# A decoder trunk on one Trainium2 core: norm weights loaded first, decay steps later, the residual's second half summed and turned by VectorE

## The chip, the cores and the metric

The kernel runs on one core of one Trainium2 chip. A core has TensorE (PE in the profile; its weight loads are listed apart as PEld), VectorE (DVE), ScalarE (ACT), GpSimd (POOL) and SyncE (SP), and 16 DMA engines, to which SP, ACT and POOL issue transfers. SBUF is the on-chip memory of 128 partitions, PSUM the memory that TensorE writes to. The metric is the device time of one execution in microseconds, as the median of several runs.

## The reference: what is computed

One layer of a decoder trunk on 1024 positions of width 1024, all in float32. Its core:

```python
h = rms_norm(x, g_mix[l])
z = jnp.einsum("bsd,de->bse", h, w_in[l]) + b_in[l]
va, ga, xb, gb, sa, sb = jnp.split(z, cuts, axis=-1)
u = va * jax.nn.sigmoid(ga)
u = causal_depthwise_conv(u, conv_a_w[l], conv_a_b[l])          # width 31
u = jax.nn.silu(layer_norm(u, ln_g[l], ln_b[l]))
y_a = jnp.einsum("bsc,cd->bsd", u, w_a_out[l])
v = causal_depthwise_conv(xb, conv_b_w[l], conv_b_b[l])         # width 4
v = rg_lru(v, w_rg_a[l], b_rg_a[l], w_rg_x[l], b_rg_x[l], lam[l])
y_b = jnp.einsum("bsc,cd->bsd", v * jax.nn.gelu(gb), w_b_out[l])
m = jax.nn.sigmoid(sa) * y_a + jax.nn.sigmoid(sb) * y_b
x = x + jnp.einsum("bsd,de->bse", m, w_o[l])

h = rms_norm(x, g_mlp[l])
f = jnp.square(jax.nn.relu(jnp.einsum("bsd,df->bsf", h, w_1[l])))
x = x + jnp.einsum("bsf,fd->bsd", f, w_2[l])
return rms_norm(x, g_final)
```

`rms_norm` divides each position by the root of its mean square (plus 1e-6) and multiplies by channel weights. The decay of the recurrence `rg_lru` needs `softplus(-lam)` for 1536 channels, which depends on the weights alone.

## The kernel before

**Layout and precision.** Activations lie with channels on the partitions and positions along the free dimension, in tiles of 128 x 1024 (two blocks of 512). Each float32 operand of a product is split into a high and a low part (`split`, `split_dma`, `low`), and a product is three matmuls: high times high, high times low, low times high. `split_dma` lets POOL form the low part by an accumulating DMA; the other two use VectorE. The larger products work in blocks of two by two with seven partial products, so that sums of blocks are formed on VectorE in between.

**Order of the work.** Nearly all of it is written out by hand: inside `tc.manual_schedule` the named engines run their instructions in the program's order. In most parts these are all five engines; in the first part (the start) and in the two parts of the MLP they are ScalarE, VectorE and TensorE only, and the order of SP and POOL is left to a scheduler. `later` puts VectorE work aside with a due time from a hand-kept clock (`clk`, advanced by `at`), and `vector_work` issues what was put aside. An engine runs its own instructions in order and waits where an input isn't there yet.

**The start (lines 107 to 422).** `vecs` is one array of 448 channel vectors of 128; its first eight are the norm weights `g_mix`. They are loaded alone into `gmix` by ACT's queue (L169), and the whole of it into `vec` by POOL (L130), behind the making of `ident` and the constants `onesm` and `ones`. `idle_mm` runs ten matmuls of `ones` on TensorE. `x_plain` (L236) multiplies a transposed x part by its norm weight and rounds it to the high part `xh`, `x_plain_low` (L240) makes the low part `xl`, and `first_z` (L274) issues the first products from them. The first half of the positions goes through TensorE without its root; for the second half `x_square` (L202 on VectorE for tile 6, L204 on ScalarE) sums the squares of rows, `x_root` (L211 and on) takes the root and forms diagonal tiles `rd`, and `x_spread` (L226) spreads them over all partitions with matmuls into `rb`. Between them `decay_on(n)` issues the next `n` of the 51 small VectorE operations of `decay` (128 x 12 elements each): 6, 14 and 5 at the start, the rest in step 5 of the first loop over output chunks (its index is `s`; each step is one output chunk of 128 channels).

**The residual and its norm (lines 1400 to 1660, steps `GX`).** The products named `a`, `o` and `u` are the convolution branch's output product, the output projection `w_o`, and the beginning of the MLP's first product. Each runs in seven groups, in the order `GORD`, of four matmul sets of twelve; `o0` is the first step of `o` and `u0 = 2 * o0` the first of `u`. The dictionary `GX` says what is issued behind the matmuls of a step. `x1[k, o, c2]` is the residual; `o` is 0 for even and 1 for odd positions, called the first and the second half here. `x1_second` makes the pieces of the second half: of group 5 (steps `o0 + 20` to `23`) and of group 3 (steps `o0 + 24` to `27`), each with one VectorE addition at the beginning of the next step.

For the first half the sums of squares go this way: `x1_sq` squares a piece on ScalarE (L1545), `x1_add` adds it up on VectorE, `x1_cols` (L1574) sums over partitions by four matmuls with a column of ones, `x1_root` and `x1_diag` take the root and make diagonal tiles, `x1_spread` (L1637) spreads them, `x1_normed` multiplies the residual by them and by the norm weights, in place. The residual is also needed as rows at the end: `x1_turn` turns it by VectorE in blocks of 32 x 32, and `x1_rows_out` writes it to `x1d` in DRAM, four DMAs a call with pieces of 512 bytes.

For the second half `x1_rows` does both: 32 transposes on TensorE (L1587) into PSUM, squares from there with the sums along the row on ScalarE (L1592), eight copies out of PSUM on VectorE (L1596), four DMAs of whole rows (L1600).

**The MLP's first product (steps `useq`, extra work in `UX`).** The block `i` of w_1 is loaded by `up_load` (L1679), its sums and splits are made by `up_lhs`, and `up_step` runs the matmuls and empties PSUM. Loads, operands, the residual and its norm all take their tiles from one pool `T` of 37 tiles of 128 x 1024.

Of the kernel before, what the change touches and what calls it, by code (L numbers as in the profile page):

```python
# [9 lines left out]
F32 = mybir.dt.float32  # L10
# [3 lines left out]
ALU = mybir.AluOpType  # L14
# [16 lines left out]
def trunk_kernel(ctx: ExitStack, tc: tile.TileContext, x, xt_in, xt_eo, vecs, w_in, w_a_out, w_b_pl, w_b_sq,  # L31
# [74 lines left out]

    ident = cp.tile([P, P], F32, name="ident")
# [4 lines left out]
    ones = cp.tile([P, P], F32, name="ones")  # L112
    nc.gpsimd.memset(ones, 1.0)
# [14 lines left out]

    gmix = cp.tile([P, 16], F32, name="gmix")
    nc.gpsimd.dma_start(vec, vecs)  # L130
# [38 lines left out]
    nc.scalar.dma_start(gmix[:, 0:8], vecs[:, 0:8])  # L169
# [8 lines left out]
    for t in range(4, 8):  # L178
        load_x(t)
    for c2 in range(4):  # L180
        load_xc(1, c2)
# [169 lines left out]
    with tc.manual_schedule(engines={mybir.EngineType.Activation, mybir.EngineType.DVE,  # L351
# [30 lines left out]
        decay_on(6)  # L382
# [4 lines left out]
        decay_on(14)  # L387
# [34 lines left out]
        nc.vector.tensor_tensor(csum, pairs[:, :, 0, :], pairs[:, :, 1, :], ALU.add)  # L422

# [405 lines left out]
    with tc.manual_schedule(engines=ENGINES):  # L829
        for s in range(3, NC1):  # L830
# [48 lines left out]
            if s == 5:  # L879
                decay_on()  # L880
# [662 lines left out]
    def x1_sq(i, m_):  # L1543
        s = EV(f"sq{i}{m_}")
        nc.scalar.activation(s, x1[i // 2, 0, i % 2][:, HALVES[m_]], AF.Square)  # L1545
        sqs.append((at("A", 0.62, clk["V"]), s))
# [6 lines left out]
    def x1_turn(kk):  # L1553
        for th in range(2):
            r = T(f"x1r{kk}{th}")
            for c2 in range(2):
                src = x1[kk, 0, c2].rearrange("p (m h b j) -> p h m b j", m=2, h=2, j=32)[:, th]
                dst = r.rearrange("p (b m j) -> p m b j", m=4, j=32)[:, 2 * c2:2 * c2 + 2]
                dve(0.65, 0, nc.vector.transpose, dst, src)
            turned.append((kk, th, r))  # L1560

    turned = []
# [15 lines left out]
    def x1_rows(*ts):  # L1578
        for t in ts:
            o, n = divmod(t, 4)  # L1580
            if n == 0:
                rst[o] = cp.tile([P, 6, 4], F32, tag="st6", name=f"stm{o}", bufs=2)
            rows = T(f"x1r{t}")
            for kk in range(2):
                ps = bank(f"tr{t}{kk}")
                for c in range(4):
                    nc.tensor.transpose(ps[:, c * P:(c + 1) * P],  # L1587
                                        x1[kk, o, c // 2][:, c % 2 * HS + n * P:c % 2 * HS + (n + 1) * P],
                                        ident)
                at("P", 0.45)  # L1590
                a = T(f"sq{t}{kk}")[:, 0:HS]
                nc.scalar.activation(a, ps, AF.Square, accum_out=rst[o][:, kk, n:n + 1])  # L1592
                at("A", 0.63, clk["P"])

                def copy(rows, kk, ps, t):
                    nc.vector.tensor_copy(  # L1596
                        rows[:, HALVES[kk]].rearrange("p (g c j) -> p c g j", g=4, c=4),
                        ps.rearrange("p (c g j) -> p c g j", g=4, c=4))
                    if kk:
                        nc.sync.dma_start(x1d[t], rows)  # L1600

                later(clk["P"], 0.63, copy, rows, kk, ps, t)
            if t == 7:
                x1_root(1)
            if o:
                vector_work(clk["V"])

    def x1_root(o):

        if o == 0:  # L1610
            rst[o] = cp.tile([P, 6, 4], F32, tag="st6", name=f"stm{o}", bufs=2)
        a, b, v, s = (rst[o][:, i, :] for i in range(4))
        if o:
            tt(v, a, b, ALU.add)
        nc.vector.tensor_scalar(v, v if o else sqs[1][:, 0:4], 1.0 / D, EPS, ALU.mult, ALU.add)
        nc.scalar.activation(s, v, AF.Sqrt)
        at("A", 1.5)
# [679 lines left out]
```

## Time and profile before

| | |
|---|---|
| Median of 3 runs | 1528.98 us (1528.98 to 1529.56) |
| The profiled execution's own time | 1529.02 us |
| Its span, first to last instruction | 1527.2 us |
| Mean granted clock of TensorE | 0.998 |
| TensorE busy | 1517.7 us |

A page of the profile lists busy times by engine, the share of 40 slices, the DMA queues, the chain of work that ended last, and the costliest groups of instructions. A row of the timeline reads: start, length, engine, line of the kernel, operation, output and inputs by tile names, shape, count, and in brackets how long the engine stood idle before it and what ended that. A tile name stands for all tiles whose name begins that way (`x1r` for `x1r00` and so on; `x` also for the tiles `x100` and the like of the residual). Helpers that record all operations have one line: L482 is `dve`, which issues most of VectorE's work in the later parts, L1236 is `low`, and L65 to L67 are `split_dma`. `SPq` and `ACTq` are DMA issues by these engines' sequencers. "us to landing" is from the issue until the last byte is in place.

### The profile page before, as it was taken

To read this page: it belongs to the slowest core of one execution; us is meant where nothing else is said; L and a number is where in the kernel's file an instruction comes from. 1 tells how busy PE (TensorE), PEld (TensorE's weight loads), DVE (VectorE), ACT (ScalarE), POOL (GpSimd) and SP (SyncE) were. 2 spreads that over 40 slices of the span, in tenths; PEclk is the share of its full clock that TensorE was granted. 3 is DMA by queue.
4 is the path that set the end of the run, shared out by engine and by line. 5 is a ranking of instruction groups with operands and counts; after the bars stand their busy time and mean duration, and the time that the engine had idled before them with its cause. 6 is when DMAs were issued, how large, how long until landed. Compare 5 with 4: busy or idle time off the path is not lost.

```text
span 1527.2 us, 18954 instructions
## 1 busy us (share of the span) xinstructions
PE 1517.7 (99%) x6712; PEld 1249.8 (82%) x6712; DVE 1200.8 (79%) x1640; ACT 927.0 (61%) x1299; POOL 192.3 (13%) x228
## 2 busy tenths in 40 slices
PE   9999999999999999999999999999999999999998
PEld 7878887888888888888888888888888888888886
DVE  7899996999999997788869879755555387777777
ACT  6749688586566657645575777554444455545475
POOL 0111011022222222000022322000000000101010
PEclk9999999999999999999999999999999999999999
DMA  9756778698997789863779897333333974776465
GB/s 352 187 145 159 176 177 191 193 260 213 266 260 173 186 207 273 292 231 121 263 205 302 186 200 189 124 126 111 111 111 111 307 261 129 187 201 167 110 123 153
DMA packets 130943, 295.48 MB, mean 193 GB/s; under 512 B 12912, under 2 KB 34928, under 8 KB 130848
## 3 DMA queue, kind: packets, MB, share of 16 engines
q1 hardware_dynamic: 98816, 214.60, 41.1%
q0 software_dynamic: 31600, 79.15, 28.2%
q8 instruction: 52, 0.85, 0.2%
q10 hardware_dynamic: 432, 0.53, 0.1%
q14 instruction: 43, 0.35, 0.1%
HBM read 148.74 MB, written 60.82 MB: 137 GB/s over the span
## 4 chain that ended last, share of the span: by engine, by line
PE 98%; DMA 1%; DVE 0%; issue 0%; SPq 0%; ACT 0%; DVEq 0%
PE z L745 16%; PE d1b L2017 2%; PE d2b L2017 2%; PE d0b L2017 2%; PE d3b L2017 2%; PE d0e L2017 1%; PE d0a L2017 1%; PE d3e L2017 1%; PE d3a L2017 1%; PE d1e L2017 1%; PE d1a L2017 1%; PE d2e L2017 1%; PE d2a L2017 1%; PE z L274 1%; PE rg L552 1%; PE rg L554 1%
## 5 line engine op out<-in xcount | busy, mean ns | idle before, releaser
L745 PE MATMUL z<-xh,win_h 128*128 128x512 f32 x368 | 115.5, 391 | 0.0
L745 PE MATMUL z<-xl,win_h 128*128 128x512 f32 x368 | 115.0, 390 | 0.0
L657 DVE SCALAR_TENSOR_TENSOR y<-u,vec,y 128x511 f32<-128x511 f32 (+14 forms) x120 | 88.2, 735 | 0.0
L745 PE MATMUL z<-xh,win_l 128*128 128x512 f32 x368 | 87.5, 390 | 0.0
L657 DVE SCALAR_TENSOR_TENSOR yt<-u,vec,yt 128x511 f32<-128x511 f32 (+6 forms) x112 | 82.4, 736 | 0.0
L657 DVE SCALAR_TENSOR_TENSOR y<-yt,csum,y 128x511 f32<-128x511 f32 (+6 forms) x112 | 82.4, 736 | 0.0
L745 PEld LDWEIGHTS z<-xh,win_h 128*128 128x128 f32 x368 | 69.1, 188 | 15.9 <-ACT win_h L67 0.5
L745 PEld LDWEIGHTS z<-xl,win_h 128*128 128x128 f32 x368 | 69.1, 188 | 14.9
L745 PEld LDWEIGHTS z<-xh,win_l 128*128 128x128 f32 x368 | 69.1, 188 | 14.6
L562 ACT ACTIVATE g<-rg,vec 96x1024 f32<-96x1024 f32 x32 | 35.5, 1110 | 72.9 <-PE rg L554 72.9
L1712 ACT ACTIVATE o<-s 128x512 fp32r<-128x512 f32 x56 | 33.7, 623 | 45.2 <-DVE s L1696 26.4
L66 POOL DMA_DIRECT2D zo<-zw x45 | 39.2, 871 | 134.7 <-ACT zo L65 116.8
L503 DVE SCALAR_TENSOR_TENSOR v<-xb,vec,v 128x1023 f32<-128x1023 f32 (+2 forms) x36 | 46.2, 1282 | 5.8 <-ACT v L494 4.9
L66 POOL DMA_DIRECT2D db_10l<-br x4 | 3.5, 876 | 338.3 <-DMA br<-in_w_dram 253.0
L66 POOL DMA_DIRECT2D win_l<-win_raw x23 | 20.0, 868 | 194.2 <-ACT win_l L65 159.4
L65 ACT ACTIVATE zo<-zw 128x512 fp32r<-128x512 f32 x45 | 28.2, 626 | 24.2 <-PE z2f L946 2.1
L1236 DVE TENSOR_TENSOR o<-s,o 128x512 fp32r<-128x512 f32 x56 | 37.3, 683 | 1.5 <-ACT o L1712 1.5
L66 POOL DMA_DIRECT2D zo<-zs x30 | 26.4, 879 | 74.9 <-ACT zo L65 62.8
L67 ACT ACTIVATE zo<-zw 128x512 fp32r<-128x512 f32 x45 | 27.9, 621 | 0.0
L598 DVE TENSOR_TENSOR_SCAN g<-a,g 128x1024 f32<-128x1024 f32 x12 | 27.5, 2291 | 0.4
L66 POOL DMA_DIRECT2D ga<-gsa x8 | 7.0, 874 | 161.0 <-DMA m<-mbd 150.8
L1236 DVE TENSOR_TENSOR o<-w_raw,o 128x512 fp32r<-128x512 f32 x38 | 25.9, 683 | 0.0
(3178 smaller groups left out, 4910.1 us busy)
## 6 DMA issues: line engine op xcount, KB each, us to landing
w_raw<-in_w_dram SPq DMA_DIRECT2D x32, 512.0 KB, 5.1
br<-in_w_dram SPq DMA_DIRECT2D x32, 512.0 KB, 5.8
ar<-fd SPq DMA_DIRECT2D x32, 512.0 KB, 6.6
zw<-in_w_in_dram SPq DMA_DIRECT2D x28, 512.0 KB, 6.9
win_raw<-in_w_in_dram SPq DMA_DIRECT2D x23, 512.0 KB, 4.6
win_l<-win_raw POOLq DMA_DIRECT2D x23, 512.0 KB, 4.8
zo<-zw POOLq DMA_DIRECT2D x45, 256.0 KB, 5.8
gates<-zg SPq DMA_DIRECT2D x32, 256.0 KB, 4.4
```

Of the source, the lines that this page charges most:

```text
L65: nc.scalar.activation(l, src, AF.Copy, scale=-1.0)
L66: nc.gpsimd.dma_start(l, src, accum_op=ALU.add)
L67: nc.scalar.activation(h, src, AF.Copy)
L274: nc.tensor.matmul(z0[i][:, HALVES[hf]], w0[i][w][:, k, :], xpart(a, hf, k), start=k == 0 and which == "hh", stop=k == 7 and which == ("hl ...
L503: nc.vector.scalar_tensor_tensor(v[:, d:S], a[:, 0:S - d], cbw_c[:, w * 12 + t:w * 12 + t + 1], v[:, d:S], ALU.mult, ALU.add)
L562: nc.scalar.activation(a, gps.pop((n, gi))[:HD, :], AF.Sigmoid, bias=(ba_c, bx_c)[gi][:, n:n + 1])
L598: nc.vector.tensor_tensor_scan(i, a, i, 0.0, ALU.mult, ALU.add)
L657: nc.vector.scalar_tensor_tensor(o[:, k:], a[:, 0:HS - k], c, o[:, k:], ALU.mult, add)
L745: nc.tensor.matmul(zps[s][:, HALVES[hf]], w[:, k, :], xw[k][part][hf], start=n == 0, stop=n == 23)
L1236: tt(l, src, h.bitcast(F32), ALU.subtract)
L1712: nc.scalar.activation(o[:, 0], src, AF.Copy)
L2017: nc.tensor.matmul(o, a, b, start=start and n == 0, stop=stop and n == len(todo) - 1, skip_group_check=not start or not stop)
```

## The change

1. `ones` is made first on POOL, and POOL then loads the norm weights into `gmix`; `ident` and `onesm` follow. ACT no longer loads them.
2. The whole of `vecs` is loaded by SP, behind x tiles 4 to 7 and ahead of the transposed x of the second part of positions.
3. The decay steps: none ahead of the first root; 5 at the end of the start, 27 in step 5, the others in step 6.
4. For the second half of the residual `x1_rows` is gone. Its squares and sums now go as those of the first half (`x1_sq`, `x1_add`, `x1_cols`), its rows by `x1_turn` in steps 12, 14, 16 and 18 of the first product, with `x1_rows_out` in steps 14 to 20.
5. The first half's rows are written right behind their turning (steps `o0 + 20` and `21`) rather than in steps 8 to 14 of the first product.
6. `x1_normed` writes the second half's result to four new tiles `hq`, so that the residual stays until it is turned.
7. `(g_parts, "u", 2, 1)` moves from step `o0 + 27` to `u0`, `(up_lhs, 0, 6)` from `u0` to `u0 + 1`.

```diff
+    ones = cp.tile([P, P], F32, name="ones")
+    nc.gpsimd.memset(ones, 1.0)
+    gmix = cp.tile([P, 16], F32, name="gmix")
+    nc.gpsimd.dma_start(gmix[:, 0:8], vecs[:, 0:8])
     ident = cp.tile([P, P], F32, name="ident")
     make_identity(nc, ident)
     onesm = cp.tile([P, P], F32R, name="onesm")
     nc.gpsimd.memset(onesm.bitcast(F32), 1.0 / D)
-    ones = cp.tile([P, P], F32, name="ones")
-    nc.gpsimd.memset(ones, 1.0)
...
-    gmix = cp.tile([P, 16], F32, name="gmix")
-    nc.gpsimd.dma_start(vec, vecs)
...
-    nc.scalar.dma_start(gmix[:, 0:8], vecs[:, 0:8])
...
     for t in range(4, 8):
         load_x(t)
+    nc.sync.dma_start(vec, vecs)
     for c2 in range(4):
         load_xc(1, c2)
...
-        decay_on(6)
...
-        decay_on(14)
...
         nc.vector.tensor_tensor(csum, pairs[:, :, 0, :], pairs[:, :, 1, :], ALU.add)
+        decay_on(5)
...
-            if s == 5:
-                decay_on()
+            if s in (5, 6):
+                decay_on(27 if s == 5 else 99)
...
-    def x1_sq(i, m_):
-        s = EV(f"sq{i}{m_}")
-        nc.scalar.activation(s, x1[i // 2, 0, i % 2][:, HALVES[m_]], AF.Square)
+    def x1_sq(i, m_, o=0):
+        if o and (i, m_) == (0, 1):
+            sqs.clear()
+        name = f"sq{i}{m_}{o}"
+        s = T(name)[:, 0:HS] if o and (i, m_) in ((0, 1), (3, 0)) else EV(name)
+        nc.scalar.activation(s, x1[i // 2, o, i % 2][:, HALVES[m_]], AF.Square)
         sqs.append((at("A", 0.62, clk["V"]), s))
...
+    def x1_turn(kk, th, o):
+        r = T(f"x1r{kk}{th}{o}")
+        for c2 in range(2):
+            src = x1[kk, o, c2].rearrange("p (m h b j) -> p h m b j", m=2, h=2, j=32)[:, th]
+            dst = r.rearrange("p (b m j) -> p m b j", m=4, j=32)[:, 2 * c2:2 * c2 + 2]
+            dve(0.65, 0, nc.vector.transpose, dst, src)
+        turned.append((kk, 2 * o + th, r))
...
-    def x1_rows(*ts):
...
             hq[kk, o, c2] = src = a = x1[kk, o, c2]
+            if o:
+                hq[kk, o, c2] = a = T(f"hq{kk}{c2}")
...
-        20: ((x1_add,), (x1_sq, 3, 1), (flush,), (x1_turn, 0)),
-        21: ((x1_add,), (flush,), (x1_cols,), (x1_turn, 1), (up_load, 0, (1,))),
+        20: ((x1_add,), (x1_sq, 3, 1), (flush,), (x1_turn, 0, 0, 0), (x1_turn, 0, 1, 0),
+             (x1_rows_out,), (x1_rows_out,)),
+        21: ((x1_add,), (flush,), (x1_cols,), (x1_turn, 1, 0, 0), (x1_turn, 1, 1, 0),
+             (x1_rows_out,), (x1_rows_out,), (up_load, 0, (1,))),
         22: ((x1_diag, 0), (up_load, 1, (1,))),
-        23: ((x1_spread, 0), (x1_normed, 0, 0)), 24: ((g_parts, "u", 1, 0), (g_parts, "u", 1, 1)),
-        25: ((x1_normed, 1, 0),), 26: ((g_parts, "u", 2, 0),), 27: ((g_parts, "u", 2, 1),)}.items()})
+        23: ((x1_spread, 0), (x1_normed, 0, 0)), 24: ((g_parts, "u", 1, 0), (g_parts, "u", 1, 1), (x1_sq, 0, 1, 1)),
+        25: ((x1_sq, 1, 1, 1), (x1_sq, 2, 1, 1), (x1_add, 2), (x1_normed, 1, 0), (x1_sq, 3, 1, 1)),
+        26: ((x1_add,), (x1_sq, 0, 0, 1), (x1_add,), (g_parts, "u", 2, 0), (x1_sq, 1, 0, 1)),
+        27: ((x1_add,), (x1_sq, 2, 0, 1), (x1_add,))}.items()})
...
-        0: ((up_lhs, 0, 6), (x1_rows, 4, 5, 6, 7)),
-        1: ((x1_diag, 1),), 2: ((x1_spread, 1), (up_lhs, 1, 6)),
+        0: ((x1_sq, 3, 0, 1), (x1_add,), (flush,), (g_parts, "u", 2, 1), (x1_cols,)),
+        1: ((x1_diag, 1), (up_lhs, 0, 6)), 2: ((x1_spread, 1), (up_lhs, 1, 6)),
...
-    UX.update({n: ((x1_rows_out,),) for n in range(8, 16, 2)})
+    UX.update({n: UX.get(n, ()) + ((x1_turn, n // 2 % 2, n // 4 - 3, 1),) for n in (12, 14, 16, 18)})
+    UX.update({n: UX.get(n, ()) + ((x1_rows_out,),) for n in (14, 16, 18, 20)})
```

More of the change, by code (lines that the diff above doesn't have):

```diff
@@ L1576, in x1_cols @@
         at("P", 0.9)
-    def x1_rows(*ts):
[L1579 to L1606, printed above, removed]
-    def x1_root(o):
[L1610 to L1615, printed above, removed]
+    def x1_root(o):
+        rst[o] = cp.tile([P, 6, 4], F32, tag="st6", name=f"stm{o}", bufs=2)
+        v, s = rst[o][:, 2, :], rst[o][:, 3, :]
+        nc.vector.tensor_scalar(v, sqs[1][:, 0:4], 1.0 / D, EPS, ALU.mult, ALU.add)
         nc.scalar.activation(s, v, AF.Sqrt)
```

10 lines of the change are left out of this document (2 added, 8 removed).

## The prediction, made before the changed kernel had run

> **What bounds the kernel now.** I read the page first: the busy times, and the chain that ended last.
>
> ```profile
> PE 1517.7 (99%) x6712; PEld 1249.8 (82%) x6712; DVE 1200.8 (79%) x1640; ACT 927.0 (61%) x1299; POOL 192.3 (13%) x228
> PE 98%; DMA 1%; DVE 0%; issue 0%; SPq 0%; ACT 0%; DVEq 0%
> ```
>
> TensorE (PE) is the bound nearly throughout: 1517.7 us for 6712 instructions, 0.226 us each. So time can come from two places: work taken off TensorE, and the few moments at which it stands still. The waits of TensorE name one that hangs on the kernel's data:
>
> ```profile
> PE rb L226 <- DVE rd L217: 0.7, 1, 0.7
> ```
>
> The chain of waits over the first 26 us (start, length, what) shows how it comes about:
>
> ```profile
> 2.12 5.91 DMA xc<-in_xt_dram
> 8.05 8.97 DMA x<-in_x_dram
> ...
> 17.05 1.23 DVE x L202 x2
> 18.28 0.09 DVE sm L302
> ...
> 22.71 1.13 PE rb L226 x8
> ```
>
> Until 17 us it runs over transfers, then over VectorE (DVE): a square of x, small decay operations (L302 and on), and only behind them the row root that feeds `rb`. From 22.71 on it is TensorE. The transfers are at their limit meanwhile (a stretch with its length, busy PE, PEld, DVE, ACT, POOL, clock, DMA share, GB/s):
>
> ```profile
> 8.05:23.80 15.75, 15.07 (x68) 11.51 (x67) 12.86 (x45) 10.36 (x18) 0.00 (x0) 1.00 1.03 411
> ```
>
> **The start.** The 224 KB of `vec` leave the head of the transfers and go to SP's queue behind x tiles 4 to 7, ahead of the second half's `xc`. At 411 GB/s 229,376 bytes are 0.56 us: what lies between lands that much earlier, what lies behind lands as before. The last x tile, its square and the root:
>
> ```profile
> 18.33 1.06 ACT L204 ACTIVATE x<-x 128x1024 f32<-128x1024 f32 x1 [1.41 <-DMA x<-in_x_dram]
> 19.30 0.19 ACT L204 ACTIVATION_READ_ACCUMULATOR x<-x 128x1 f32 x1
> 20.77 0.16 DVE L211 TENSOR_SCALAR stx<-stx 128x4 f32<-128x4 f32 x1
> ```
>
> ScalarE (ACT) squares the tile as it lands and has the sum at 19.49; the root starts at 20.77, because decay operations stand ahead of it on VectorE. They go away. The root then starts at 19.49 - 0.56 + 0.05 = 19.0, and `rb`, 1.94 us behind it now (22.71 - 20.77), could start at 20.9.
>
> TensorE's own work then decides:
>
> ```profile
> 12.21 0.19 PEld L274 LDWEIGHTS z<-xl,w_h 128*128 128x128 f32 x1 [0.45 <-DVE xl L240]
> ...
> 22.71 1.13 PE L226 MATMUL rb<-rd,ones 128*128 128x128 f32 x8 [0.67 <-DVE rd L217]
> ```
>
> Its last matmul ahead of `rb` ended 0.67 us before 22.71, at 22.04; as a matmul of 0.39 us is followed by the next after 0.23, TensorE was ready at 21.88. The small stall at 12.21 is one of two of its kind; each hangs on an x part that lands 0.56 us earlier now. I take 0.5 us out for both. The beginning hangs on the norm weights:
>
> ```profile
> 1.35 0.20 POOL L113 MEMSET ones<- 128x128 f32 x1
> 1.54 0.71 POOL L130 DMA_DIRECT2D vec<-in_vecs_dram  x1
> ...
> 5.37 1.33 ACT L236 ACTIVATE xh<-xc,gmix 128x512 fp32r<-128x512 f32 x2 [0.42 <-DMA gmix<-in_vecs_dram]
> ```
>
> ```profile
> vec<-in_vecs_dram POOLq DMA_DIRECT2D x1, 224.0 KB, 5.7
> gmix<-in_vecs_dram ACTq DMA_DIRECT2D x1, 4.0 KB, 4.1
> ```
>
> ScalarE waits 0.42 us for `gmix`, whose landing 4.1 us after its issue on ACT's queue releases 5.37. With the change POOL issues it right behind the memset of `ones`, which now comes ahead of two memsets and a select on POOL: some 0.6 us earlier than `vec` is issued now, at 0.95. No row shows what 4 KB take from POOL. At 4.1 us it lands at 5.05, 0.25 earlier than now; at the 5.7 us of `vec` at 6.65, 1.35 later. I take 4.25, near the row of its own size, and so 0.1 us earlier. `ident` and `onesm` come some 0.7 us later on POOL; `ident` is first used near 22 us. [...]
>
> `rb` starts at 21.88 - 0.5 - 0.1 = 21.3, later than the 20.9 of VectorE, so TensorE is what decides. **The start gains 22.71 - 21.3 = 1.4 us**; bounds 0.0 (weights at 6.65) and 1.8 (VectorE's 20.9). All that follows moves along.
>
> **The moved decay steps.** Of 51 operations 25 ran at the start and 26 near 64 us; now 5 follow `csum`, 27 stand in step 5 and 19 in step 6. That puts 20 x 0.2 us = 4 us more on a full VectorE behind 64 us. It runs off behind the convolution steps; the next one that another engine needs is
>
> ```profile
> 111.35 3.92 DVE L503 SCALAR_TENSOR_TENSOR v<-xb,vec,v 128x1023 f32<-128x1023 f32 x3 [0.69 <-ACT v L494]
> 119.70 1.05 ACT L65 ACTIVATE vtl<-v 128x1024 fp32r<-128x1024 f32 x1
> ```
>
> It ends at 115.3, 4.4 us ahead of ScalarE's need; the 0.69 us of idle time takes up a part of the 4. I cost it at nothing. If the cover were gone, ScalarE's later splits would slip by as much, at most 4 us.
>
> **The residual's second half: what TensorE saves.** 32 transposes go, four column sums of the kind that the first half has come in their place:
>
> ```profile
> 887.80 0.95 PE L1574 MATMUL cs<-ones,sq 128*128 128x1 f32 x8
> 888.61 0.49 PE L1442 MATMUL go2e<-go5h,go 128*128 128x512 f32 x1
> ...
> 908.70 3.65 PE L1587 MATMUL tr<-ident,x 128*128 128x128 f32 x32
> 912.11 0.48 PE L1442 MATMUL gu1a<-gu1h,gu 128*128 128x512 f32 x1
> ```
>
> From start to next start 3.41 against 0.81 us: 2.60 us off TensorE.
>
> **What it costs there.** The transposes needed only the residual. The column sums need the squares of all eight pieces, added up, and stand in TensorE's order at the same place, 908.70. The last piece, `x<-xe,go3e`, can be squared only when VectorE has made it, and VectorE gets six of the seven additions ahead of it:
>
> ```profile
> 901.39 2.72 DVE L482 SCALAR_TENSOR_TENSOR x<-x,vec,rbm 128x512 f32<-128x512 f32 x4
> ...
> 906.18 0.69 DVE L482 TENSOR_TENSOR x<-xe,go3e 128x512 f32<-128x512 f32 x1 [0.88 <-PE go3e L1442]
> ```
>
> ```profile
> 883.34 0.63 ACT L1545 ACTIVATE sq<-x 128x512 f32<-128x512 f32 x1 [0.69 <-DVE x L482]
> ```
>
> VectorE was free at 906.18 - 0.88 = 905.30. Six additions at 0.68 us (2.72 / 4) are 4.1 us: the last piece starts at 909.4 instead of 906.18 and is done at 910.1. Its square (0.1 to hand over, 0.63) is done at 910.8, the seventh addition (0.05 + 0.69) at 911.6. TensorE waits 911.6 - 908.7 = 2.9 us, and nothing can pass it there, since its order is fixed. So **this part is +0.3 us** (2.9 - 2.6). Additions at 0.62 us make 911.2 of it, and -0.1; if ScalarE's two copies of 0.62 for the next weights get ahead of the square, it is +1.5. A gain isn't excluded: with no wait it is -2.6. The chain behind (root, diagonal, spread) has two groups of twelve matmuls, 5.4 us, to pass in, as it had. The eight copies out of PSUM that VectorE loses came behind 910 and don't help ahead of it.
>
> Two steps come later: the split of the `u` product's second operand by one group (two copies on ScalarE, one POOL transfer; used three groups on, 8 us) and the sums for the first w_1 block (two on VectorE, two copies, one POOL transfer; used 20 us on). The first half's 16 row writes now have a place in SP's order, ahead of two w_1 loads that ran between them; these aren't read before those sums.
>
> **The turning, later.** Eight transposes of 0.62 us go to steps 12 to 18 of the first product, two in two steps of 2.7 us, and 16 row writes to SP's queue in place of four:
>
> ```profile
> 883.76 2.49 DVE L482 STREAM_TRANSPOSE x1r<-x 128x512 f32<-128x512 f32 x4
> ```
>
> ```profile
> 960.00:975.00 15.00, 15.00 (x68) 12.42 (x67) 11.08 (x18) 8.52 (x12) 0.00 (x0) 1.00 0.23 90
> ```
>
> VectorE has 3.9 us free in 15, the transfers more than that: hidden, 0. Without that cover each pair could cost its 1.25 us, 5 us in all.
>
> **Sum.** -1.4 + 0.3 = -1.1 us, against the profiled execution's own time of 1529.02 us (span 1527.2 and 1.8 around it; the median is 1528.98, so nothing is to be shifted): **1527.9 us**. For itself it reaches from 1526.6 to 1529.5.
>
> **Rivals.**
> - *The sums are in time.* If VectorE's additions fit in between and TensorE waits little, the 2.6 us come in full: 1529.02 - 1.4 - 2.6 = 1525.0. For it: VectorE's 0.88 us of idle time just there. Against it: the six additions need 4.1.
> - *Buffers run short (slower).* Four more 4 KB-wide tiles (the normed copies), and the residual itself until its last turn, sit in the pool of 37 that w_1 loads and left operands come from. One load then has a small margin:
>
> ```profile
> 978.98 1.25 SPq L1679 DMA_DIRECT2D w_raw<-in_w_dram  x2
> 983.80 1.14 ACT L1712 ACTIVATE o<-w_raw 128x512 fp32r<-128x512 f32 x2
> 986.59 0.39 PE L1724 MATMUL f4a<-gu1h,o 128*128 128x512 f32 x1
> ```
>
> The block is copied at 983.80 and, with 0.62 + 0.69 us for its two parts, is ready by 985.4; TensorE needs it at 987.05: 1.6 us. If the load must wait for a tile that the last turn frees (step 18, near 983), it is 4 us late and TensorE stands for 2.4: 1527.9 + 2.4 = 1530.3, slower than before from a delay of 2.7 us on. If it waits for the row writes to land as well, 5 us more: 1535. For it: four tiles are much where each part of an operand takes one of the 37. Against it: by then the operands of the first steps are used up.
> - *The weights come late*, so that "norm weights first" isn't what happens. At 6.65 the start gains 0.0, and the rest stays: 1529.3. For it: the only POOL load of that time took 5.7 us. Against it: it had 56 times the bytes.
> - *The standing TensorE slows down.* The first 20 matmuls of the kernel run at a slow pace:
>
> ```profile
> 1.60 4.64 PE L361 MATMUL spare<-ones 128*128 128x128 f32 x20 [1.60 <-POOL ones L113]
> ```
>
> That is 0.23 us each, where the transposes of the same size take 3.41 / 32 = 0.107: 2.5 us lost in 20. If the wait of 2.9 us brings that back, it is 1527.9 + 2.5 = 1530.4. Against it: no wait of that length in the middle of the kernel shows it. [...]
>
> **How the numbers follow.** Forecast 0.54, sums in time 0.17, buffers 0.14, late weights 0.11, slow pace 0.04. The time is that of the forecast. About 0.2% (3.06 us around 1528.98: 1525.9 and 1532.0) is what a measurement of this kernel tells from no change. Faster: nearly all of the second case and a little of the first, 0.19. Slower: the worse half of the buffer case and what I haven't seen, 0.11. Same: 0.70. The range reaches to the sums in time below and to the milder buffer case above, with 0.2 and 0.9 us for their own spread: 1524.8 to 1531.2.
>
> **What would show it.** `rb` starts near 21.3 with no wait for `rd`, and `xh` at 5.2 to 5.4. The column sums of the second half stand 2 to 3.5 us behind the group ahead of them, and wait for VectorE's last addition; `x<-xe,go3e` then no longer waits for TensorE. Between 65 and 120 us and from 930 on TensorE shows no gap. I am wrong if the weights land behind 6 us, if the sums wait under 1 us, or if a w_1 load ends a wait of TensorE.

## The result, and the profile after

The changed kernel takes 1534.28 us (median of 7 runs, 1533.58 to 1535.76) against 1529.43 us for the kernel before in the same session (7 runs, 1528.98 to 1530.11): a ratio of 1.0033, 95% interval 1.0023 to 1.0043. It is 4.85 us slower. 1527.9 was forecast, and the time lies above the range. The profiled execution took 1534.28 us with a span of 1532.5, so 5.3 us more span than before.

Where the time goes is read from TensorE's start on the same groups of matmuls in both timelines, since TensorE is the bound: a difference that grows between two groups was lost there. (In the tables a group is named by its bank and the operand's part, as in the profile.)

| TensorE's start of | before, us | after, us | difference |
|---|---|---|---|
| `z<-xh,win_h`, at 54 us | 54.10 | 53.55 | -0.55 |
| `go2e<-go5` (behind the first half's sums) | 888.61 | 888.26 | -0.35 |
| `gu0a<-gu2` (behind the second half's sums and spread) | 921.28 | 924.38 | +3.11 |
| `f1d<-gu7` (MLP) | 945.79 | 948.86 | +3.07 |
| `f1d<-gu4` | 956.67 | 961.15 | +4.48 |
| `f3b<-gu6` | 972.99 | 978.60 | +5.61 |

Behind that nothing changes for TensorE: at 1141 us it is still 5.60. So there are three places: the start gains little, the column sums lose 3.5, and the first MLP products lose 2.5. TensorE's waits of after between 900 and 980 us name the last two (before had none in this stretch):

```profile
PE cs L1574 <- DVE sq L480: 2.7, 1, 2.7
PE f0d L1693 <- DVE gu4l L1234: 0.8, 1, 0.8
PE f2c L1693 <- ACT fb L1741: 0.4, 1, 0.4
```

**The column sums.** The wait is the one that was forecast, at its place and nearly at its length. TensorE's timeline:

```profile
908.12 0.39 PE L1440 MATMUL gu0a<-gu1h,gu 128*128 128x512 f32 x1
911.18 1.86 PE L1574 MATMUL cs<-ones,sq 128*128 128x1 f32 x8 [2.67 <-DVE sq L480]
912.91 0.77 PE L1440 MATMUL gu1a<-gu1h,gu 128*128 128x512 f32 x1
913.48 0.63 PE L1440 MATMUL gu1a<-gu1l,gu 128*128 128x512 f32 x1
```

and VectorE's, which makes the last piece and the last addition:

```profile
909.06 0.68 DVE L480 TENSOR_TENSOR x<-xe,go3e 128x512 f32<-128x512 f32 x1
910.44 0.69 DVE L480 TENSOR_TENSOR sq<-sq,sq 128x512 f32<-128x512 f32 x1 [0.69 <-ACT sq L1546]
```

From 908.12 a matmul is followed after 0.23 us, so TensorE stood from 908.35 to 911.18: 2.83 us, where 2.9 were forecast. What was not forecast stands behind it: the eight small matmuls take 1.73 us to the next start (912.91 - 911.18) instead of 0.81, and the next product's matmuls follow one another after 0.43 us, not 0.23. The clock says why (a stretch, its length, busy PE, PEld, DVE, ACT, POOL, clock, DMA share, GB/s):

```profile
905.50:908.30 2.80, 2.80 (x14) 2.16 (x12) 2.70 (x5) 2.20 (x4) 0.96 (x2) 1.00 1.14 230
908.30:911.10 2.80, 0.21 (x1) 0.00 (x0) 2.00 (x4) 2.47 (x5) 0.86 (x1) 0.98 1.06 202
911.10:914.50 3.40, 3.32 (x12) 3.03 (x13) 1.02 (x7) 2.90 (x6) 1.06 (x2) 0.50 1.00 187
914.50:917.90 3.40, 3.40 (x10) 2.63 (x9) 3.30 (x7) 1.87 (x5) 1.26 (x2) 0.51 0.82 147
917.90:921.00 3.10, 3.10 (x17) 2.58 (x16) 0.37 (x2) 2.72 (x6) 1.12 (x2) 1.00 0.55 96
```

The granted clock is 0.50 for 6.8 us behind the pause, and 1.00 again from 917.9.

**The MLP's first products.** The waits for `gu4l` and `fb` are the end of a chain that begins on SP's queue. What that queue waited for between 935 and 980 us, in after:

```profile
SPq L1648 <- DMA o<-w_raw: 10.6, 1, 10.6
```

and in before, where the same loads of w_1 stand on line 1679:

```profile
SPq L1679 <- DVE gu3l L1236: 4.2, 1, 4.2
SPq L1679 <- DVE gu7l L1236: 3.6, 1, 3.6
```

A load waits for a free tile. Before, `gu7l` at 941.4 frees one:

```profile
941.42 4.98 SPq L1679 DMA_DIRECT2D w_raw<-in_w_dram  x2
```

After, none is free until a copy of an earlier w_1 block has landed, and the load is issued at 951.52. VectorE, in order, then stands 2.5 us for it with `gu4l` queued behind:

```profile
955.49 0.69 DVE L1664 TENSOR_TENSOR s<-w_raw 128x512 f32<-128x512 f32 x1 [2.50 <-DMA w_raw<-in_w_dram]
```

**The start.** Between the loads and the root (ScalarE's square of the last x tile, VectorE's first step of the root), and the same two pieces of the chain of waits as before:

```profile
18.74 1.06 ACT L203 ACTIVATE x<-x 128x1024 f32<-128x1024 f32 x1 [1.43 <-DMA x<-in_x_dram]
```

```profile
19.92 0.17 DVE L210 TENSOR_SCALAR stx<-stx 128x4 f32<-128x4 f32 x1 [1.24 <-ACT x L203]
```

```profile
2.12 6.31 DMA xc<-in_xt_dram
...
22.43 0.89 PE rb L225 x8
```

The root now follows the square at once (19.92 instead of 20.77), but the tile has landed no earlier (18.74 against 18.33 before), and the first whole `xc` tile, issued at 2.12, takes 6.31 us instead of 5.91. In TensorE's timeline the first matmul for `rb` starts at 22.27 without a wait, where before had 22.71 and 21.3 was forecast.

### The profile page after: what moved, and what is told of

Its sections match the earlier page's. It is cut to its first block, busy times and chain, and to the rows that moved or that the text cites. A ratio compares the mean times of both kernels' runs of the same rounds, so it can differ in the third digit from the quotient of the medians.

```text
span 1532.5 us, 18931 instructions
## 1 busy us (share of the span) xinstructions
PE 1519.8 (99%) x6688; PEld 1248.8 (81%) x6688; DVE 1205.1 (79%) x1646; ACT 927.8 (61%) x1291; POOL 190.2 (12%) x228
## 4 chain that ended last, share of the span: by engine, by line
PE 97%; DVE 1%; ACT 1%; issue 1%; DMA 0%; SPq 0%; ACTq 0%; DVEq 0%
PE z L743 16%; PE d1b L1993 2%; PE d2b L1993 2%; PE d0b L1993 2%; PE z L273 2%; PE d3b L1993 2%; PE d0e L1993 1%; PE d0a L1993 1%; PE d3e L1993 1%; PE d3a L1993 1%; PE d2e L1993 1%; PE d2a L1993 1%; PE d1e L1993 1%; PE d1a L1993 1%; PE rg L550 1%; PE rg L552 1%
## 5 line engine op out<-in xcount | busy, mean ns | idle before, releaser
L65 ACT ACTIVATE zo<-zw 128x512 fp32r<-128x512 f32 x45 | 28.2, 626 | 24.3 <-PE z10f L944 2.1
L1681 ACT ACTIVATE o<-w_raw 128x512 fp32r<-128x512 f32 x38 | 23.6, 621 | 6.0 <-DMA w_raw<-in_w_dram 6.0
```

The lines of the kernel that those rows point to most:

```text
L65: nc.scalar.activation(l, src, AF.Copy, scale=-1.0)
L1681: nc.scalar.activation(o[:, 0], src, AF.Copy)
```

## The experiments

Each kernel but the fifth, which was only profiled, was timed against the kernel before. Ratios are to the kernel before; after itself is 1.0033. One table serves them all: TensorE's start less that of before's profile, us. One profile of each kernel stands in it, and the first column differs by up to 1.0 us among kernels that are the same up to there (before and run 6 by 0.56). So a row is read by how it changes from column to column.

| run | `go2e` (sums 1) | `gu0a<-gu2` (sums 2) | `f1d<-gu7` | `f1d<-gu4` | `f3b` |
|---|---|---|---|---|---|
| after | -0.35 | +3.11 | +3.07 | +4.48 | +5.61 |
| after again (5) | -0.46 | +1.51 | +3.05 | +5.24 | +6.33 |
| matmuls in the pause (1) | -0.56 | -0.20 | +1.35 | +2.65 | +3.72 |
| sums a step later (2) | +0.38 | -2.00 | +2.66 | +4.90 | +6.02 |
| turned early (3) | -0.04 | +0.31 | +3.05 | +3.06 | +3.06 |
| before, four tiles held (6) | +0.56 | +0.58 | +1.57 | +2.81 | +3.49 |
| order of S4, S3 (7) | -0.65 | -0.30 | +1.22 | +2.37 | +3.47 |
| later, spread early (8) | +0.20 | +1.60 | +1.64 | +5.41 | +5.76 |
| all together (9) | +0.13 | -0.38 | +0.58 | +0.59 | +2.73 |

### 1. Matmuls in the pause

```diff
+    x1_done = [False, True]
...
         sqs.append(bank("cs"))
+        if x1_done.pop(0):      # second half only
+            for n in range(12):
+                nc.tensor.matmul(sqs[1][:, 0:P], ones, ones, start=True, stop=True)
```

> The kernel after, with twelve matmuls of 128 columns (ones by ones, into the bank of the column sums) put on TensorE in front of the second half's column sums, so that TensorE computes during its 2.83 us wait; nothing else changes. Theory 1 (the pause itself lowered the granted clock to 0.50): the clock stays at 1.00, the column sums take 0.8 us instead of 1.7 and the next product 2.7 us instead of 5.1, so about 3.3 us less than after: 1531.0, and rows of 0.23 us for that product. Rival (the slow matmuls come from something that VectorE or a transfer does then, or the buffers later on set the time anyway): the product keeps 0.43 us a matmul, or the gain is given back before the MLP, and the time stays at 1534.3 within 0.5.

Measured: 1532.76 us (1532.09 to 1533.92), 1.0020 [1.0011, 1.0029]. The stretch that was at 0.50 is at full clock:

```profile
908.30:911.10 2.80, 2.80 (x25) 2.61 (x25) 1.92 (x3) 2.48 (x5) 0.86 (x1) 1.00 1.07 208
911.10:914.50 3.40, 3.40 (x20) 2.94 (x20) 1.79 (x9) 3.30 (x8) 1.72 (x2) 1.00 1.10 206
```

All 11 executions of this kernel have a mean granted clock of 0.999, the 8 of after (run 5 included) 0.997 or 0.998. So in after the pause is what lowers the clock. At the sums the kernel stands at -0.20: the exchange of transposes for a wait costs 0.36 us there (from -0.56), against the 0.3 forecast. But only 1.8 of the 3.3 us reach the end (4.85 us slower than before became 3.06): 1.6 come back at the first MLP products, where VectorE now holds TensorE up. Its timeline shows one reason:

```profile
919.87 0.69 DVE L1673 TENSOR_TENSOR s<-w_raw,w_raw 128x512 f32<-128x512 f32 x1 [2.42 <-ACT u L1494]
920.48 5.35 DVE L480 SCALAR_TENSOR_TENSOR hq<-x,vec,rbm 128x512 f32<-128x512 f32 x8
```

A difference for w_1 (the second of two, called S4 and S3 from here on) stands ahead of the normed halves and waits 2.4 us. In after this wait was hidden by TensorE's own lateness.

### 2. The sums a step later

```diff
-        0: (..., (g_parts, "u", 2, 1), (x1_cols,)),
-        1: ((x1_diag, 1), (up_lhs, 0, 6)), 2: ((x1_spread, 1), (up_lhs, 1, 6)),
-        3: ((x1_normed, 0, 1), ...
+        0: (..., (g_parts, "u", 2, 1)),
+        1: ((x1_cols,), (up_lhs, 0, 6)), 2: ((x1_diag, 1), (up_lhs, 1, 6)),
+        3: ((x1_spread, 1), (x1_normed, 0, 1), ...
...
-            elif n == u0 + 1:
+            elif n == u0 + 2:
                 x1_root(1)
```

> The kernel after, with the second half's column sums one step later (after the next product of 2.7 us), and root, diagonal and spread one step later with them. Theory 1 (wait of 2.83 us plus half a clock behind it): TensorE loses neither the wait nor the 3.3 us of slow matmuls, about 5.9 us less: 1528.4, with a wait of under 0.5 us at the column sums. Rival (the root, the diagonal and the normed halves are the chain that sets the first MLP product, and come one step of 2.7 us later in the order): a new wait of 1 to 2.7 us at the first MLP product, 1529.5 to 1531.1. Buffers alone: unchanged, 1534.3.

Measured: 1533.76 us (1532.69 to 1535.24), 1.0027 [1.0017, 1.0037]. At the sums it does what theory 1 says: no pause, TensorE 2.4 us better than at the first half's sums. All of it is lost by `f1d<-gu7`, and 2.3 us besides: the waits are for `gu6h`, `gu6l` and `gu7l`, which come from the normed halves. The rival was right in kind, and larger than it said.

### 3. Turned early, no tiles held

```diff
-            if o:
-                hq[kk, o, c2] = a = T(f"hq{kk}{c2}")
...
-        1: ((x1_diag, 1), (up_lhs, 0, 6)), 2: ((x1_spread, 1), (up_lhs, 1, 6)),
+        1: ((x1_diag, 1), (up_lhs, 0, 6), (x1_turn, 0, 0, 1), (x1_turn, 0, 1, 1), (x1_rows_out,), (x1_rows_out,)),
+        2: ((x1_spread, 1), (up_lhs, 1, 6), (x1_turn, 1, 0, 1), (x1_turn, 1, 1, 1), (x1_rows_out,), (x1_rows_out,)),
...
-    UX.update({n: UX.get(n, ()) + ((x1_turn, n // 2 % 2, n // 4 - 3, 1),) for n in (12, 14, 16, 18)})
-    UX.update({n: UX.get(n, ()) + ((x1_rows_out,),) for n in (14, 16, 18, 20)})
```

> The kernel after, with the second half turned by VectorE in the two steps behind the diagonal, and its rows written out there, so that the norm is taken in place and no four tiles are held until the MLP's first product. Theory 2 (the tiles held make the loads of w_1 wait 10 us for a free tile, and TensorE stalls 2.4 us at 958 to 976 us): the loads are issued 5 us or more earlier against the step, those stalls go, 2.4 us less than after: 1531.9. Rival (VectorE's 5.3 us of turning is the load, wherever it lies): it has 2.7 us idle there, so the normed halves come 2.6 us later and the first MLP product waits 1 to 2 us instead: 1533.4 to 1536.

Measured: 1531.72 us (1530.78 to 1533.03), 1.0014 [1.0005, 1.0023]. Both sides showed. From `f1d<-gu7` on the row of the table stays at 3.06: the late loads are gone. And VectorE's turning costs 2.7 us ahead of that, at 933 to 948 us, as TensorE's waits say:

```profile
PE cs L1574 <- DVE sq L480: 2.7, 1, 2.7
PE f0d L1691 <- DVE gu7l L1234: 1.0, 1, 1.0
PE f0b L1691 <- DVE gu6l L1234: 0.9, 1, 0.9
```

The column sums waited as long as in after, and yet the clock did not fall:

```profile
908.60:911.40 2.80, 0.22 (x1) 0.00 (x0) 2.00 (x4) 2.48 (x5) 0.86 (x1) 1.00 1.05 203
911.40:914.80 3.40, 3.30 (x19) 2.89 (x20) 1.61 (x10) 3.40 (x8) 1.66 (x2) 1.00 1.06 197
```

That the time comes within 0.2 us of theory 2's 1531.9 is therefore in part luck: the full clock and VectorE's turning, neither of them in that sum, work against each other. In other executions of this kernel the mean clock says that it did fall: the six with a mean granted clock of 0.998 took 1530.8 to 1531.7 us, the five with 0.995 to 0.997 took 1532.4 to 1533.0.

### 5. After once more

> The kernel after once more, for its profile alone. TensorE's pause ahead of the second half's column sums was 2.83 us in the profile of after, with half a clock behind it, and 2.84 us in the run that turns early, with a full clock behind it. If the length of the pause decides, this run shows 0.43 us a matmul again and a span near 1532.5. If it is chance whether a pause of this length is followed by half a clock, it may show 0.23 us a matmul and then a span of 1531 (the 3.3 us of slow matmuls less what comes back later, 1.9 us in the run with matmuls in the pause).

One run, 1535.01 us, span 1533.2. The same pause, and half a clock for one stretch of 3.4 us instead of two:

```profile
908.20:911.00 2.80, 0.20 (x1) 0.00 (x0) 2.00 (x4) 2.48 (x5) 0.86 (x1) 1.00 1.07 208
911.00:912.40 1.40, 1.32 (x10) 1.28 (x11) 0.19 (x2) 1.40 (x3) 0.86 (x1) 0.99 1.10 199
912.40:915.80 3.40, 3.40 (x10) 2.64 (x9) 2.79 (x10) 2.25 (x7) 0.86 (x2) 0.50 1.00 188
```

Neither sentence of the expectation held whole: after the same pause the clock was halved for 6.8, 3.4 and 0 us in three executions. At the sums this run is 1.6 us better than the first profile of after; at `f1d<-gu7` both stand at 3.05. What the clock loses there, VectorE would have lost a little later.

### 6. The kernel before, with four tiles held

```diff
+    def hold():
+        for n in range(4):
+            a = T(f"hold{n}")
+            nc.vector.memset(a[:, 0:1], 0.0)
+            held_t.append(a)
...
-        3: ((x1_normed, 0, 1), ...
+        3: ((hold,), (x1_normed, 0, 1), ...
...
+    UX.update({16: ((let_go,),), 18: ((let_go,),)})
```

> The kernel before, with four more tiles of its largest pool taken at the step that takes the second half's norm and let go at the MLP's steps 16 and 18 (eight tiny VectorE instructions of some 0.1 us); nothing of the change. Theory 2 (the tiles held are what stalls TensorE 2.4 us at the MLP's first products): the loads of w_1 there are issued 10 us later as in after, TensorE stalls about 2.4 us, 1532.1 against 1529.7. Rival (VectorE's turning and sums are what is late there): no stall, 1529.7 within 0.4.

Measured: 1532.88 us (1532.16 to 1533.92), 1.0020 [1.0011, 1.0028]: 3.25 us lost with nothing of the change in it. SP's queue waits as in after, and TensorE behind it:

```profile
SPq L1679 <- DMA o<-w_raw: 10.5, 1, 10.5
```

```profile
PE f0d L1724 <- DVE gu4l L1236: 0.8, 1, 0.8
PE f0d L1724 <- DVE gu7l L1236: 0.7, 1, 0.7
PE f2c L1724 <- ACT fb L1772: 0.4, 1, 0.4
```

By the table 1.9 us of it lie behind `f1d<-gu7` and are the late loads. The 1.0 at `gu7l` is something else: in this kernel too the differences S4 and S3 came out ahead of the normed halves, which start at 920.70 instead of 918.76 (0.56 of that is the kernel's later beginning). So late loads of w_1 cost some 2 us by themselves.

### 7. S4 and S3 behind the normed halves

```diff
-        7: (..., (g_t, "u", 0, 3), (g_t, "u", 1, 3))
+        7: (..., (g_t, "u", 0, 3), (g_t, "u", 1, 3), (up_lhs, 0, 7))
...
-    ready = 4
+    ready = 5
```

(with the twelve matmuls of the first run)

> The kernel after with the twelve matmuls in the pause (as in the earlier run), and with two VectorE instructions (the differences S4 and S3 of the first rows of w_1, of which S3 waits 2.4 us for ScalarE there) put behind the normed halves instead of ahead of them. Theory 3 (with TensorE 3.3 us earlier, the normed halves held back by S3 are what gives 1.6 us back at the MLP's first products): the normed halves start at 918.1 instead of 920.5, the waits of 0.3 and 1.1 us go, 1531.2 against 1532.8. Rival (VectorE and ScalarE are full there whatever the order): 1532.8 within 0.4.

Measured: 1532.18 us (1531.93 to 1533.63), 1.0017 [1.0008, 1.0026]. The normed halves start at 918.45, as meant, and still `f1d<-gu7` stands at +1.22 (1.35 without); the time is 0.6 us below the first run's, where 1.6 were expected. Theory 3 falls as far as its size goes: VectorE picks the two instructions up later instead, and idles 0.87 and 0.61 us for others in between.

```profile
930.43 1.23 DVE L1234 TENSOR_TENSOR gu6l<-gt2u,gu6h 128x1024 fp32r<-128x1024 f32 x1 [0.87 <-ACT gu6h L1384]
938.74 0.69 DVE L1673 TENSOR_TENSOR s<-w_raw,w_raw 128x512 f32<-128x512 f32 x1 [0.61 <-DMA o<-s]
```

In before the two fill the first of these gaps:

```profile
928.57 0.68 DVE L1698 TENSOR_TENSOR s<-w_raw,s 128x512 f32<-128x512 f32 x1
929.17 1.22 DVE L1236 TENSOR_TENSOR gu6l<-gt2u,gu6h 128x1024 fp32r<-128x1024 f32 x1
930.31 0.68 DVE L1700 TENSOR_TENSOR s<-w_raw,w_raw 128x512 f32<-128x512 f32 x1
```

From the first normed half to the second `gu7l` VectorE takes 24.28 us there, 24.12 in run 1 and 26.03 here. So the order matters, and the rival (full whatever the order) isn't shown either; before's order with the matmuls in the pause wasn't run.

### 8. Sums later, spread early

```diff
-        1: ((x1_diag, 1), (up_lhs, 0, 6)), 2: ((x1_spread, 1), (up_lhs, 1, 6)),
+        1: ((x1_cols,), (up_lhs, 0, 6)), 2: ((x1_diag, 1), (x1_spread, 1), (up_lhs, 1, 6)),
...
-            elif n == u0 + 1:
+            elif n == u0 + 2:
                 x1_root(1)
```

(with run 7's two lines for S4 and S3, without its matmuls)

> The kernel after with the column sums one step later, the diagonal in the step behind and the spread right behind it (so the normed halves do not come later), and S4 and S3 behind the normed halves. Theory 1 and 3 together: no pause and no half clock (5.9 us less at the column sums), no wait at the MLP's first products beyond 0.5 us, the buffers' 2.4 us still there: 1528.4 to 1529.5. Rival (VectorE full from 915 to 950 us): 1 to 3 us of new waits at the first MLP products, 1530 to 1532.

Measured: 1532.90 us (1531.78 to 1534.44), 1.0020 [1.0010, 1.0029]. Not what either theory gave: the spread waited for its diagonal, because the square root stood on ScalarE's queue behind six other instructions. VectorE's next step shows it:

```profile
916.02 0.18 DVE L98 RECIPROCAL stm<-stm 128x4 f32<-128x4 f32 x1 [2.94 <-ACT stm L1583]
```

A pause of 2.0 us at 915.6, and two of 1.5 and 1.0 us from 957.0 on, were followed by half a clock:

```profile
915.10:918.50 3.40, 1.56 (x12) 1.16 (x10) 2.27 (x9) 2.62 (x7) 1.72 (x2) 0.98 1.03 180
918.50:921.90 3.40, 3.40 (x10) 2.73 (x10) 3.36 (x6) 2.67 (x5) 1.43 (x2) 0.51 0.77 130
921.90:925.00 3.10, 3.10 (x15) 2.51 (x15) 3.10 (x5) 0.60 (x1) 0.29 (x1) 1.00 0.91 154
956.00:959.40 3.40, 1.64 (x7) 0.78 (x5) 2.42 (x4) 2.48 (x4) 0.00 (x0) 0.99 0.00 1
959.40:962.80 3.40, 3.02 (x7) 2.44 (x8) 3.40 (x7) 1.98 (x5) 0.00 (x0) 0.50 0.20 77
```

### 9. All together

```diff
-        1: ((x1_diag, 1), (up_lhs, 0, 6)), 2: ((x1_spread, 1), (up_lhs, 1, 6)),
+        1: ((x1_cols,), (x1_root, 1), (up_lhs, 0, 6)),
+        2: ((x1_diag, 1), (x1_spread, 1), (x1_turn, 0, 0, 1), (x1_turn, 0, 1, 1), (up_lhs, 1, 6)),
...
-            elif n == u0 + 1:
-                x1_root(1)
...
-            if o:
+            if o and kk:
                 hq[kk, o, c2] = a = T(f"hq{kk}{c2}")
...
-    UX.update({n: ... (x1_turn, n // 2 % 2, n // 4 - 3, 1),) for n in (12, 14, 16, 18)})
+    UX.update({n: ... (x1_turn, 1, (n - 8) // 2, 1),) for n in (8, 10)})
```

(the row writes move along, to steps 5 and 6 of `u` and to steps 10 and 12)

> The kernel after with the column sums one step later, the square root queued on ScalarE right behind them (in the run before it waited 2.9 us behind splits), diagonal and spread in the next step, the first two of the four turnings in front of the norm, in place, and the last two at the MLP's steps 8 and 10, so that two tiles are held instead of four. All theories together: no pause over 0.5 us at the column sums and at most 1 us at the spread, so no half clock, TensorE 1.5 to 2.5 us ahead of before at the step behind; the loads of w_1 wait less, under 0.7 us of stalls at the MLP; VectorE no earlier than before at the normed halves (918.4 at best against 918.8), so 0.5 to 1.5 us of waits at the first MLP products. Sum with the start's 0.5: 1527.3 to 1529.0 against 1529.6. Rival (VectorE full from 903 to 950 us gives all of it back, whatever the order): 1529.5 to 1531.

Measured: 1531.11 us (1530.48 to 1532.88), 1.0012 [1.0003, 1.0021]: the best of the versions with the second half on VectorE, and still slower than before. Of the 2.6 us that TensorE is relieved of, 0.5 are left at `gu0a<-gu2` (it waits 1.3 us for the diagonal), and at 970 us VectorE is behind by the last two turnings (1.3 us each) and a w_1 load that it waits 0.7 us for, with two tiles still held:

```profile
PE f2c L1693 <- DVE fa L1719: 1.9, 1, 1.9
PE rbm L1604 <- ACT rdm L1596: 0.9, 1, 0.9
```

### 4, 10, 11, 12. The start alone

All four are the kernel before with a part of the start. In 4 and 12 it is the whole start, in 10 the decay steps alone, in 11 the loads alone:

```diff
-        decay_on(6)        # 4, 10, 12
-        decay_on(14)       # 4, 10, 12
+        decay_on(5)        # 4, 10, 12: behind csum
...
-    nc.gpsimd.dma_start(vec, vecs)                        # 4, 11, 12
-    nc.scalar.dma_start(gmix[:, 0:8], vecs[:, 0:8])       # 4, 11, 12
+    nc.gpsimd.dma_start(gmix[:, 0:8], vecs[:, 0:8])       # 4, 11, 12
+    nc.sync.dma_start(vec, vecs)                          # 4, 11, 12: behind x tiles 4 to 7
```

> The kernel before, with the start of the kernel after alone (norm weights first and on GpSimd's queue, channel vectors behind the first loads, decay steps later). By the prediction's step for the start 1.4 us less than before: 1528.0. By the trace of after, where TensorE runs 0.55 us ahead at 54 us and 0.35 us at 888 us: 1529.1. If the loads of x come 0.4 us later and it matters: 1529.8.

> The kernel before with the decay steps alone moved away from the first root. If the start's gain is VectorE's queue ahead of the root (25 small instructions of 0.06 to 0.1 us), this keeps it: 0.5 us less than before, 1529.1, with the spread of the first norm at 22.2 instead of 22.7 us. If it is the channel vectors behind the loads (the prediction's larger term), this shows nothing: 1529.6. The kernel with the whole start on the before measured 1528.7.

> The kernel before with the loads' part of the start alone: norm weights first on GpSimd's queue, channel vectors behind x tiles 4 to 7; the decay steps where they were. Prediction's step: everything behind 7 us lands 0.56 us earlier and the norm weights 0.1 us, so 0.7 us less than before. From the profiles so far, where the last of the first four x tiles lands at 18.1 to 18.7 us with the vectors behind it and at 18.3 to 18.7 with them ahead: nothing, 1529.5 within 0.4, and the spread of the first norm 4.4 us behind that landing, as in before. If decay operations now wait for the late vectors in front of the root: up to 1 us more, 1530.5.

> The kernel before with the whole start once more, for a second interval beside the loads' part alone. By the first run of it 1.0 us less than before (1528.5 against 1529.5); by the decay steps' run 0.6 less (1528.9).

| run | time, us | before, us | ratio, interval |
|---|---|---|---|
| 4, whole start | 1528.71 | 1529.70 | 0.9993 [0.9984, 1.0002] |
| 12, whole start | 1529.17 | 1530.09 | 0.9993 [0.9984, 1.0002] |
| 10, decay steps alone | 1528.88 | 1529.48 | 0.9996 [0.9987, 1.0005] |
| 11, loads alone | 1535.10 | 1530.09 | 1.0039 [1.0025, 1.0053] |

The whole start measured 0.9 to 1.0 us less twice, with intervals that still include 1. It is the fastest version here. The decay steps alone measured 0.6 less, with an interval that includes 1 too. Their run shows what they change: the last x tile landed later than in before (squared from 19.16, where before had 18.33), and the root followed 1.2 us behind that instead of 2.4:

```profile
19.16 1.06 ACT L204 ACTIVATE x<-x 128x1024 f32<-128x1024 f32 x1 [1.41 <-DMA x<-in_x_dram]
```

```profile
20.34 0.17 DVE L211 TENSOR_SCALAR stx<-stx 128x4 f32<-128x4 f32 x1 [1.24 <-ACT x L204]
```

The spread, expected at 22.2, started at 22.71 as in before, but now without a wait for the root: TensorE itself came to it no earlier in this execution.

The loads alone cost 5.0 us, five times the worst that was expected: the decay operations, still ahead of the root in VectorE's order, now wait for vectors that land at 19.1.

```profile
19.13 0.17 DVE L288 TENSOR_SCALAR sm<-vec 128x12 f32<-128x12 f32 x1 [4.78 <-DMA vec<-in_vecs_dram]
...
24.98 0.17 DVE L210 TENSOR_SCALAR stx<-stx 128x4 f32<-128x4 f32 x1
```

```profile
PE rb L225 <- DVE rd L216: 4.7, 1, 4.7
```

This pause of 4.7 us, too, is followed by half a clock: 0.50 is granted from 25.8 to 32.6 us, and the mean granted clock of the five executions is 0.996 to 0.998, where before has 0.998 or 0.999.

So in the change the decay steps had to move because the vectors did. By the medians most of the gain comes from them; that the loads add the rest isn't shown.

## Why the prediction was wrong, step by step

Three terms failed: the turning as "hidden, 0", which left out the tiles that are held until it runs; the small chance of a slowed TensorE; and the start's size. The range took the rivals one at a time. Two of them came together, and 1527.9 with both prices (2.5 and 2.4) is 1532.8, outside it.

**The start, -1.4 us: right in sign, too large, and its larger term was wrong.** "At 411 GB/s 229,376 bytes are 0.56 us: what lies between lands that much earlier" failed. In the eleven profiles with the vectors behind the x tiles the last of these tiles landed at 18.1 to 18.7 us; in the three with the vectors ahead of them at 18.3, 18.7 and 19.1. The means lie 0.2 us apart, less than either group's own spread. The 411 GB/s were read from a window that begins at 8.05 us, when the vectors had landed already (7.25), and said nothing of the stretch in which they run. The small stalls that were to vanish with the earlier landings (0.5 us) stayed, in other places. What held is the root: VectorE's decay operations left it, 20.77 became 19.92, and TensorE then decides, as was said. But TensorE is ready for `rb` at 22.27, not at 21.3; in the ten profiles with the whole start `rb` begins at 21.7 to 23.1, with a mean of 22.4, against 22.7 and 23.1 in before and run 6. The norm weights came neither early nor late: POOL issued them at 1.31 and not at 0.95, and they landed 4.0 us later, at 5.31, where 4.25 was taken. In time the whole start is worth 0.9 us, which its intervals don't tell from nothing.

**The moved decay steps, 0: nothing speaks against it.** TensorE's lead of 0.55 us at 54 us is 0.35 at 888, and no wait for VectorE stands between.

**TensorE's relief of 2.60 us and the wait of 2.9: right.** The wait was 2.83 us, and the run without a change of clock puts the exchange at 0.36 us against 0.3.

**"The standing TensorE slows down", 0.04: this happened.** Its price was near (2.5 us; 3.3 measured at the place, of which 1.8 reach the end). What failed is the argument against it: "no wait of that length in the middle of the kernel shows it" looked past the kernel's end: in before TensorE's last matmul ends at 1520.0 and the clock falls at 1522.6, after 2.6 us. The mean over the last stretch is 0.77:

```profile
1517.30:1527.20 9.90, 2.72 (x12) 1.90 (x11) 4.34 (x16) 3.30 (x8) 0.00 (x0) 0.77 0.46 180
```

What stands ahead of a fall of the clock can be read too. In after it falls at 911.01 us, rises at 917.84 and falls again at 1528.82, behind the last matmul. In the 3.41 us ahead of its two falls (half of the 6.83 between the first two times) TensorE is busy for 0.91 and 0.21 us, in before ahead of the one at 1522.6 for 0.82; in run 8 it is busy for 1.56 and 1.64 of the 3.40 us ahead of the slow stretches. So the clock fell though TensorE had worked for up to 1.6 us of them. Nor was little work always followed by a fall: in run 3 TensorE is busy for 0.7 of the 3.4 us from 908.1 to 911.5, and the clock stays. The same pause was followed by 6.8, 3.4 and 0 us of half clock, so its length alone doesn't tell what it costs.

What else decides isn't shown. An estimate from the times of the changes: 917.84 less 911.01 is 6.83 us and 1528.82 less 917.84 is 610.98, which are 2 and 179 times 3.41; the one slow stretch of run 5 lasts 3.4 us, and the two of run 8 begin 40.9 us apart (918.5 and 959.4), 12 times 3.41. If the clock changes only at such steps, the cost of a pause depends on where it lies between them.

**Buffers run short, 0.14: this happened too, earlier than was looked for.** The prediction priced the load behind 978 us, with a margin of 1.6 us, and argued that "by then the operands of the first steps are used up". The load that ran late was the one ahead of it, at 941, when the operands weren't. Run 6 gives it without the change: 1.9 us of stalls behind `f1d<-gu7`, and 3.25 in time with the order that came with it. The forecast's step "the turning, later: hidden, 0" fell with it, since it counted VectorE's free time and not the tiles.

**What no case had: the way from the normed halves to `gu7l`.** The prediction counted VectorE's additions up to the column sums and its free time at 960 to 975, and nothing between. In before the second `gu7l` starts at 943.04 and the matmuls on `gu7` begin at 943.07, so little is to spare. From the first normed half to that `gu7l` it takes 24.1 to 24.3 us, and 26.0 in runs 7 and 8, whatever TensorE did ahead of it. In the eight numbered runs of the table `f1d<-gu7` stands 0.21 or 0.22 us less behind than the second `gu7l` does (run 1: 1.35 and 1.56). So what starts the normed halves late comes out there: 920.48 us in run 1, 921.80 in run 2 and 922.06 in run 3, where before has 918.76. Busy time alone doesn't say it: of the 47 us from 903 to 950 VectorE is busy for 42.1 in before and for 39.3 to 39.9 in runs 1, 2 and 7, which wait more; only runs 3 and 9, with the turning in front, have more, 43.1 and 43.4.

Whether the rival "the sums are in time", 1525.0, was to be had stays open. Run 2 had them in time, but a step later, and took 1533.8; no run starts the normed halves earlier than 918.45.

**The sum.** Start -0.9, exchange +0.4, half a clock +1.8 (after less run 1, each against its own before), and what is left of 4.85, some 3.6, for the MLP's first products, where run 1's own profile shows 3.92 (from -0.20 to +3.72).

## What to carry to other kernels

Work that goes from the bound engine to a nearly idle-looking one is paid in three currencies: its time there, the wait for its result, and the tiles that are held until it runs; count all three up to the next consumer, not only at the place of the edit. On a bound TensorE fill a pause of 2 us or more with matmuls, or let a product pass it (here pauses of 2.0 and 2.8 us were followed by half a clock in after and in runs 5 and 8, not in run 3), and then see which chain bounds next. And before taking bytes off the head of a queue as time, look whether that part of the queue runs at the rate that is used.

## What had not been expected of the hardware

The granted clock fell to 0.50 after single pauses of 2.0 and 2.8 us, and after two of 1.5 and 1.0, in the middle of a busy kernel, for 3.4 or 6.8 us, and in one execution with the same 2.8 us not at all. What decides between these wasn't tried by moving the pause on purpose. In after the first half of the slow stretch (911.01 to 914.42 us) holds the column sums, which are matmuls of one column; why the clock stays at 0.50 behind it, though TensorE is busy for 3.2 us of it, stays open.

The first whole `xc` tile took 5.5 to 6.3 us in the eleven profiles with the vectors out of its way, and 5.9, 6.2 and 6.7 in the three with them in it: no gain shows. What holds the first 7 us of transfers stays open.
